# Reading three chunks of x once, transposed, instead of twice, in a fused decoder layer on one core

## The chip, the cores and the metric

The kernel runs on one core of a Trainium2 chip. The core has a matrix engine (PE in the profile, with its weight loads as PEld), VectorE (DVE), ScalarE (ACT), GpSimd (POOL), and SyncE (SP), which here only issues DMAs. The metric is the device time of one execution in microseconds (us). A trace of the profiled execution gives the span from the first to the last instruction; the execution's own time is a little longer.

## The reference

One decoder layer over 2048 rows of 1024 values, all in f32. Cut to what matters here:

```python
u = rmsnorm(h, norm_g)                 # x * rsqrt(mean(x*x) + 1e-6) * gain, row by row
proj = jnp.einsum('bsd,de->bse', u, w_in)      # 1024 -> 4096 columns
a_q, a_f, a_i, a_g, b_q, b_k, b_v, b_g = split(proj)      # 8 x 512
o_a = head_rmsnorm(hgrn2(...), ...) * silu(a_g)           # group A: 4 heads
o_b = head_rmsnorm(stick_breaking(b_q, b_k, b_v), ...) * silu(b_g)   # group B: 8 heads
h = h + concat(o_a, o_b) @ w_out
h = h + sigmoid(rmsnorm(h) @ w_ple_gate) * rmsnorm(p @ w_ple_proj)
return rmsnorm(h, final_norm)
```

The change touches the first line only: the root mean square of each row of x, and the normalised x in the layout that the projection wants.

## The kernel before

**Tiles and units.** The rows of x stand reversed in memory, in NC = 4 chunks of 512 rows (CH), each of CB = 4 blocks of 128. The projection's 4096 columns stand as 8 groups of 512 (B and A in turn). The main loop (L825) goes over 32 units, one group and one chunk each, group by group and the chunks from 3 down to 0. So units 0 to 3 are group 0 of B on chunks 3, 2, 1, 0: they need the four chunks of normalised x one after the other, and every later unit finds them all ready. All values go to the PE as two f16 parts, high and low: `xh[c]`, `xl[c]` for x, `w.h`, `w.l` for weights (shown as wh and wl). One product is then three matmuls, xh with wh, xl with wh, xh with wl (`passes`, L347). Per unit these are 48 matmuls of 512 columns for two transposed outputs (`proj_t`, here q and k) and 96 of 256 columns for two natural ones (`proj_n`, here v and the gate), all summed in PSUM tiles called pj (three of them).

**Normalising a chunk.** A chunk is held as 8 slices, k = 0 to 7, each of 128 values of the model dimension on the partitions and 512 rows along the free dimension. Chunk 3 has a path of its own (`prep_first`, L263), which the change leaves alone; its last block goes through two DMA transposes (L222, xh<-kq_t and xl<-fa_t). Chunks 2, 1 and 0 go through `prep_x` (L224):

- The chunk is read in natural order, 8 tiles of 256 KB (L230). ACT squares each and sums along the row in the same instruction (L231, with an instruction that reads the accumulator), and one DVE reduction (L243) gives `ss`, a sum for each row.
- `rsqrt` (L79) makes v on DVE (L83) and raises it to -1/2 on POOL (L84). The result has rows on the partitions and must be spread over all partitions: DVE scales the identity with it (dg, L247) and four f32 matmuls of a matrix of constants with dg (L251, 128 columns each) put it into the PSUM tile `bc`, which ACT copies to SBUF (L253).
- The chunk is read again, transposed, as 4 pairs of slices of 512 KB (L238, tag kq, two buffers), and each slice is multiplied (DVE, L258), rounded to f16 (ACT, L259) and subtracted for the low part (L260, DVE for even k, POOL for odd).

**What sets the order.** The generators are tasks. `spawn` puts one on a list with a unit by which it must be done; `run` advances tasks between the matmuls of a unit by an estimated clock, and `drain` finishes what is due. Unit 0 spawns `prep_x` for chunks 2 and 1, unit 1 for chunk 0 (L829): each chunk's task starts at least one unit ahead of the unit that uses it. The order in which each engine gets its instructions is then settled by the scheduler when the program is built; on the chip every engine takes its own in that order, and waits where an operand or a buffer is not ready. SP issues all DMAs in order from one queue.

**What runs beside it.** Every B unit spawns a mixer task (`mix_B`, L593), four blocks of it. A block has score matmuls z (from q, kept in qs_t, and keys in bkv, both written by 64 KB DMAs from SBUF to SBUF, L448 and L457, after the unit's q and k are split), two sigmoids (ACT, L616 and L617), a scan (DVE, L621, 642 long), a product (L626), f16 parts (ACT L629, POOL L631 and L633), a DMA transpose (L635, at_t<-wt_t) and output matmuls op. Each unit also loads and splits two slices of the next group's weights (L128, L132, L133).

The tags of `prep_x` in the change (kq, fa, kp0, kp1, sc, raw) are buffers that the kernel has already; the mixer of group A uses kq, fa, kp0 and kp1 from unit 4 on.

## Time and profile before

| what | value |
|---|---|
| median of 3 runs | 1259.12 us (1257.2 to 1259.24) |
| profiled execution, own time | 1259.13 us |
| its span | 1257.4 us |
| busy: PE, DVE, ACT, POOL | 96%, 69%, 47%, 28% of the span |
| mean granted PE clock | 0.987 of full speed |
| HBM read | 60.83 MB |

The shares are means over stages that differ. In the profile each engine has its own rows, and a row says how long it was busy and what ended the idle time ahead of it. A wait counts for the end only on the engine that is never idle afterwards; here that is the PE. A granted clock of 1.00 is the PE's 2.4 GHz; its other level is 1.2 GHz.

### The profile page before, as it was taken

The numbers are of one execution on the slowest core, as the hardware profiler recorded it, in microseconds if no ns is written. First come the engines' busy times: TensorE is split into PE (matmuls) and PEld (weight loads), VectorE is DVE, ScalarE is ACT, GpSimd is POOL, SyncE is SP. The second block draws the span as 40 slices with busy tenths as digits, with TensorE's granted clock in tenths as the row PEclk, the third lists the DMA queues.
The fourth block names the chain that finished last, engine by engine and source line by source line (L and its number), as shares of the span: only waits on it lengthen the run. The fifth ranks groups of instructions, "written<-read, shape, count | busy, mean of one in ns | idle before, by whom it ended". The sixth has DMA issues, their size and how long they took to land.

```text
span 1257.4 us, 25854 instructions
## 1 busy us (share of the span) xinstructions
PE 1211.4 (96%) x9802; PEld 775.9 (62%) x9802; DVE 870.4 (69%) x1736; ACT 596.4 (47%) x1507; POOL 355.0 (28%) x472
## 2 busy tenths in 40 slices
PE   7978999999999999999999999898999999999997
PEld 7655667667766777677677766665544444444443
DVE  5769799976589995579997558998854434344233
ACT  7556544544454454464454445564533333333222
POOL 4247451114442112444111444110021211111212
PEclk9999999999999999999999999899999999999999
DMA  9896731156661035772126565357644536336211
GB/s 258 260 224 172 173 106 32 41 149 145 152 147 29 19 116 145 156 179 54 27 67 142 133 156 116 129 161 200 139 82 117 151 84 162 106 108 145 59 51 53
DMA packets 258468, 155.42 MB, mean 124 GB/s; under 512 B 181280, under 2 KB 226336, under 8 KB 258336
## 3 DMA queue, kind: packets, MB, share of 16 engines
q1 hardware_dynamic: 258192, 153.43, 49.1%
q8 instruction: 79, 1.29, 0.4%
q14 instruction: 53, 0.43, 0.1%
q10 hardware_dynamic: 144, 0.26, 0.1%
HBM read 60.83 MB, written 33.55 MB: 75 GB/s over the span
## 4 chain that ended last, share of the span: by engine, by line
PE 71%; DVE 11%; DMA 9%; ACT 4%; issue 3%; POOL 2%; SPq 1%; POOLq 0%; DVEq 0%; ACTq 0%
PE pj L160 35%; PE np L160 28%; PE op L160 3%; PE lps L160 2%; DVE wl L133 2%; PE z L160 2%; DMA at_t<-wt_t 2%; DVE e_t L621 1%; DMA at_t<-kp_t 1%; DMA raw_t<-w_in 1%; DMA raw_t<-x_nat 1%; DVE kq_t L511 1%; ACT wh L132 1%; DMA raw_t<-w_out 1%; DVE e_t L626 1%
## 5 line engine op out<-in xcount | busy, mean ns | idle before, releaser
L160 PE MATMUL pj<-wh,xh 128*128 128x256 f16 x1024 | 282.1, 275 | 2.0 <-DVE ql_t L77 2.0
L160 PE MATMUL pj<-wh,xl 128*128 128x256 f16 x1024 | 282.1, 275 | 0.0
L160 PE MATMUL pj<-wl,xh 128*128 128x256 f16 x1024 | 282.0, 275 | 0.0
L160 PEld LDWEIGHTS <-xh 128*128 128x128 f16 x2048 | 201.6, 99 | 28.3 <-issue 0.3
L160 PE MATMUL pj<-xh,wh 128*128 128x512 f16 (+1 forms) x560 | 197.0, 363 | 4.4 <-ACT xh L76 2.2
L160 PE MATMUL pj<-xl,wh 128*128 128x512 f16 (+1 forms) x560 | 197.5, 362 | 2.3 <-DVE xl L260 1.7
L160 PE MATMUL pj<-xh,wl 128*128 128x512 f16 (+1 forms) x560 | 197.4, 362 | 0.0
L84 POOL TENSOR_TENSOR rs_y<-rs_v,mhalf 128x1 f32<-128x1 f32 (+2 forms) x87 | 77.4, 891 | 288.9 <-DVE rs_v L83 288.0
L160 PE MATMUL np<-wh,fy 128*128 128x512 f16 x512 | 156.4, 379 | 0.2 <-DVE e_t L732 0.2
L160 PEld LDWEIGHTS <-wh 128*128 128x128 f16 x1120 | 100.4, 98 | 88.5 <-issue 6.8
L160 PEld LDWEIGHTS <-at_t 128*128 128x128 f16 x1688 | 100.4, 98 | 84.7 <-DMA at_t<-wt_t 14.2
L160 PEld LDWEIGHTS <-fy 128*128 128x128 f16 x768 | 74.2, 98 | 87.9 <-issue 0.6
L160 PEld LDWEIGHTS <-xl 128*128 128x128 f16 x1024 | 101.2, 99 | 17.7 <-issue 2.5
L160 PE MATMUL np<-wh,at_t 128*128 128x512 f16 (+2 forms) x264 | 98.0, 373 | 0.0
L160 PE MATMUL np<-wl,at_t 128*128 128x512 f16 (+2 forms) x264 | 98.0, 373 | 0.0
L160 PE MATMUL np<-wh,wt_t 128*128 128x512 f16 (+2 forms) x264 | 97.9, 373 | 0.0
L160 PE MATMUL np<-wl,fy 128*128 128x512 f16 x256 | 97.1, 379 | 0.0
L621 DVE TENSOR_TENSOR_SCAN e_t<-e_t,reset 128x642 f32<-128x642 f32 x56 | 85.4, 1524 | 15.8 <-ACT e_t L616 15.2
L629 ACT CAST wt_t<-e_t 128x640 f16<-128x640 f32 (+1 forms) x64 | 44.7, 698 | 104.7 <-DVE e_t L626 88.8
L160 PEld LDWEIGHTS <-wl 128*128 128x128 f16 x560 | 54.0, 99 | 59.4 <-issue 2.7
L631 POOL TENSOR_TENSOR wt_t<-e_t,wt_t 128x512 f16<-128x512 f32 (+1 forms) x64 | 78.0, 1218 | 33.5 <-ACT wt_t L629 32.9
L764 DVE TENSOR_TENSOR e_t<-e_t,kq_t 128x512 f32<-128x512 f32 (+2 forms) x33 | 22.2, 674 | 92.7 <-POOL kq_t L763 92.6
(193 smaller groups left out, 2270.9 us busy)
## 6 DMA issues: line engine op xcount, KB each, us to landing
raw_t<-w_in SPq DMA_DIRECT2D x61, 256.0 KB, 3.8
raw_t<-x_nat SPq DMA_DIRECT2D x56, 256.0 KB, 3.9
y_d<-y_t SPq DMA_DIRECT2D x32, 256.0 KB, 2.6
yn<-y_d SPq DMA_DIRECT2D x16, 512.0 KB, 4.0
out<-y_t SPq DMA_DIRECT2D x31, 256.0 KB, 2.1
kq_t<-x_t SPq DMA_DIRECT2D x12, 512.0 KB, 5.1
bkv<-kn_t SPq DMA_DIRECT2D x64, 64.0 KB, 2.3
bkv<-ql_t SPq DMA_DIRECT2D x64, 64.0 KB, 2.0
```

What stands on the lines that cost most here:

```text
L84: nc.gpsimd.tensor_tensor(y, v, mhalf[:, 0:n], op=ALU.pow)
L132: nc.scalar.activation(self.h[:, k, :], self.r[k], AF.Copy, scale=g)
L133: nc.vector.scalar_tensor_tensor(self.l[:, k, :], self.r[k], g, self.h[:, k, :], op0=ALU.mult, op1=ALU.subtract)
L160: nc.tensor.matmul(out_, lhsT, rhs, start=start, stop=stop)
L511: nc.vector.tensor_tensor(act, act, other, op=ALU.mult)
L621: nc.vector.tensor_tensor_scan(fl(pr_), fl(f), fl(reset), 0.0, op0=ALU.mult, op1=ALU.max)
L626: nc.vector.tensor_tensor(sg[:, :, :w_], sg[:, :, :w_], pr_[:, :, :w_], op=ALU.mult)
L629: nc.scalar.copy(wt[:, :, :w_], sg[:, :, :w_])
L631: nc.gpsimd.tensor_tensor(wt[:, :, 3 * P : 3 * P + lw], sg[:, :, :lw], wt[:, :, :lw], op=ALU.subtract)
L764: nc.vector.tensor_tensor(h_, h_, p_, op=ALU.add)
```

## The change

`prep_x` no longer reads the natural rows. It loads all 8 transposed slices of a chunk (two pairs into kq, four single slices into fa, fa, kp0, kp1), squares each on ACT, and adds the squares into two accumulators of 128 x 512 (tag sc), even k on DVE and odd k on POOL; one more DVE add joins them. A row's sum now lies across the partitions, so four matmuls with the accumulator's blocks as weights and one column of the constant matrix (L249, one output column each) bring it to the layout that `rsqrt` wants, in the first four columns of `bc`. The constant in that matrix is a power of two, which the scale of `rsqrt` takes out. From there on the steps are the same, except that all 8 slices are in SBUF already. Chunk 2's task starts in unit 0, as before; chunk 1's is spawned when chunk 2's is through, and chunk 0's after chunk 1's.

```diff
     def prep_x(c):
-        ss = small("ssx", CB, 2)
-        hs_ = small("ssx2", 2 * CB, 2)
+
+        xt = {}
+        for k in (0, 2):
+            pair = f32("kq", (P, 2, CH))
+            nc.sync.dma_start(pair, x_t[c, :, k : k + 2, :])
+            xt[k], xt[k + 1] = pair[:, 0, :], pair[:, 1, :]
+        for k in range(4, KD):
+            xt[k] = f32(("fa", "fa", "kp0", "kp1")[k - 4])
+            nc.sync.dma_start(xt[k], x_t[c, :, k, :])
+            yield 0.5
+        acc = []
+        for k in range(KD):
+            sq = f32("sc") if k < 2 else raw("sq")
+            nc.scalar.activation(sq, xt[k], AF.Square)
+            if k < 2:
+                acc.append(sq)
+            else:
+                (nc.gpsimd if k % 2 else nc.vector).tensor_tensor(acc[k % 2], acc[k % 2], sq, op=ALU.add)
+            yield 0.8
+        nc.vector.tensor_tensor(acc[0], acc[0], acc[1], op=ALU.add)
+        yield 2.0
+        bc = pa("bc")
+        ss = bc[:, 0:CB]
         for b in range(CB):
-            for hf in range(2):
-                xn = raw("xn")
-                nc.sync.dma_start(xn, x_rows(c, b, hf))
-                nc.scalar.activation(xn, xn, AF.Square, accum_out=hs_[:, 2 * b + hf : 2 * b + hf + 1])
-            yield 1.0
...
-        r = rsqrt(ss, CB, 1.0 / D, EPS)
+            nc.tensor.matmul(ss[:, b : b + 1], acc[0][:, b * P : (b + 1) * P], ones[:, 0:1], start=True, stop=True)
+        r = rsqrt(ss, CB, 1.0 / D * p2(-SX), EPS)
...
+        if c > 0:
+            spawn(prep_x(c - 1), 0.0, -1)
...
-        for n in ([c - 1, c - 2] if u == 0 else [c - 2]):
-            if g == 0 and n >= 0:
-                spawn(prep_x(n), 0.0 if n == c - 1 else 12.0, 1)
+        if u == 0:
+            spawn(prep_x(c - 1), 0.0, 1)
```

The scheduler's order moves with it. Two places matter; in all of them names carry buffer numbers. From the PE's first matmul of unit 4 on, the order on the PE is the same in both kernels.

PE, before: the broadcast of chunk 1's factors (bc_770) stands among the first projection matmuls of unit 1, which work on chunk 2 (xh_514, xl_515); chunk 1 itself (xh_783) comes into use only with unit 2, some 260 rows further on.

```order
L160 MATMUL pj_898<-xh_514,wh_126 128x512
L251 MATMUL bc_770<-dg_738,ones_89 128x128
L251 MATMUL bc_770<-dg_772,ones_89 128x128
L160 MATMUL pj_839<-xl_515,wh_126 128x512
L160 MATMUL pj_839<-xh_514,wl_127 128x512
...
L251 MATMUL bc_770<-dg_775,ones_89 128x128
L251 MATMUL bc_770<-dg_778,ones_89 128x128
...
L160 MATMUL pj_1232<-xh_783,wh_126 128x512
```

PE, the change: the same chunk's sums (L249) and factors (bc_983) stand in the last quarter of unit 1's projection (pj_1011 is its last tile), and the second half of the factors behind a score tile of unit 1's own mixer (z_1183); only score matmuls stand between it and the first matmul of unit 2 (pj_1152, on chunk 1 as xh_1048).

```order
L249 MATMUL bc_983<-ones_89,sc_t_806 128x1 x4
L160 MATMUL pj_1011<-wl_127,xh_673 128x256
...
L256 MATMUL bc_983<-dg_1037,ones_89 128x128
...
L160 MATMUL z_1183<-bkv_318,qs0_t_753 128x128
...
L256 MATMUL bc_983<-dg_1040,ones_89 128x128
L256 MATMUL bc_983<-dg_1043,ones_89 128x128
L160 MATMUL z_1184<-bkv_318,qs1_t_754 128x128
...
L160 MATMUL z_1384<-bkv_317,qs1_t_754 128x320
L160 MATMUL pj_1152<-xh_1048,wh_126 128x512
```

What moved: the spreading of chunk 1's factors went from the head of unit 1 to its end, so the matmuls that used to stand between it and chunk 1's first use are now ahead of it. Chunk 0, with bc_1420 and unit 3, stands in the same way; chunk 2's factors stand at the very end of unit 0.

DVE, before: chunk 1's first slices (kq_t_729, low part xl_784) among the scans (L624, L626) of unit 0's mixer, ahead of the splits of unit 1's q.

```order
L258 TENSOR_TENSOR y_t_787<-kq_t_729,sc_t_781 128x512
L258 TENSOR_TENSOR y_t_805<-kq_t_729,sc_t_781 128x512
L624 SCALAR_TENSOR_TENSOR e1_t_845<-e1_t_845,reset_311 128x129
L260 TENSOR_TENSOR xl_784<-y_t_787,xh_783 128x512
L626 TENSOR_TENSOR e0_t_844<-e0_t_844,e1_t_845 128x2x128
L258 TENSOR_TENSOR y_t_811<-kq_t_731,sc_t_781 128x512
L77 SCALAR_TENSOR_TENSOR ql_t_836<-pj_839,qh_t_835 128x512
```

DVE, the change: chunk 1's first slices (kq_t_760, low part xl_1049) stand behind the splits of unit 1's outputs (bkv_319, gs_t_913), and two full scans (L627) with a product (L632) stand between the first multiplication and the first low part.

```order
L253 TENSOR_SCALAR dg_1043<-ident_84,rs_y_989 128x128
L77 SCALAR_TENSOR_TENSOR bkv_319<-pj_1011,bkv_319 128x256
L262 TENSOR_TENSOR y_t_1050<-kq_t_760,sc_t_1046 128x512
L262 TENSOR_TENSOR y_t_1082<-kq_t_760,sc_t_1046 128x512
L388 SCALAR_TENSOR_TENSOR gs_t_913<-pj_1011,gs_t_913 128x256
L627 SCALAR_TENSOR_TENSOR e1_t_1180<-e1_t_1180,reset_311 128x642
L627 SCALAR_TENSOR_TENSOR e1_t_1289<-e1_t_1289,reset_311 128x642
L632 TENSOR_TENSOR e0_t_1179<-e0_t_1179,e1_t_1180 128x640
L264 TENSOR_TENSOR xl_1049<-y_t_1050,xh_1048 128x512
```

What moved: the multiplications of a chunk went from one unit ahead of its use to the moment of its use, and the first low part stands behind 642-long scans.

## Rows read from the trace of the kernel before

**Rows 1.** Busy time by stretch (units 0 to 3, the rest); count in brackets; clock, DMA share.

```profile
12.44:46.44 34.00, 29.56 (x329) 27.62 (x329) 19.97 (x45) 25.48 (x67) 7.81 (x11) 0.90 0.92 262
46.44:73.55 27.11, 23.82 (x176) 16.63 (x174) 23.93 (x36) 16.11 (x41) 10.14 (x12) 1.00 0.88 240
73.55:106.25 32.70, 29.06 (x222) 19.97 (x220) 22.02 (x32) 17.51 (x42) 15.85 (x17) 0.90 0.81 195
106.25:141.22 34.97, 28.25 (x258) 19.50 (x256) 27.98 (x31) 17.38 (x39) 23.72 (x31) 0.95 0.67 165
141.22:1257.40 1116.18, 1093.21 (x8782) 685.08 (x8779) 770.98 (x1584) 511.65 (x1305) 287.56 (x373) 0.99 0.46 112
```

**Rows 2.** PE's waits from 0 to 142 us: total, times, longest.

```profile
PE op L160 <- DMA at_t<-wt_t: 9.0, 4, 3.3
...
PE pj L160 <- DMA xh<-kq_t: 2.2, 1, 2.2
PE pj L160 <- DVE ql_t L77: 2.0, 1, 2.0
...
PE z L160 <- DMA bkv<-ql_t: 1.6, 1, 1.6
```

**Rows 3.** Stretches in which the granted clock was low (the third last column).

```profile
30.00:36.30 6.30, 4.62 (x39) 4.27 (x39) 1.09 (x5) 1.29 (x4) 0.14 (x1) 0.73 0.85 259
91.50:98.00 6.50, 6.45 (x46) 5.14 (x47) 3.59 (x6) 3.23 (x7) 0.14 (x2) 0.53 0.77 219
128.30:132.00 3.70, 3.63 (x31) 2.86 (x32) 1.96 (x2) 3.02 (x7) 2.10 (x5) 0.54 0.70 142
```

**Rows 4.** DMA issues from 0 to 150 us: KB each, median us to landing.

```profile
raw_t<-x_nat SPq DMA_DIRECT2D x24, 256.0 KB, 4.4
...
bkv<-ql_t SPq DMA_DIRECT2D x16, 64.0 KB, 2.2
```

**Rows 5.** ACT's groups from 0 to 140 us, by form: busy, mean ns, idle before.

```profile
L231 ACT ACTIVATE raw_t<-raw_t 128x512 f32<-128x512 f32 x24 | 15.1, 631 | 12.9 <-DMA raw_t<-x_nat 12.9
...
L616 ACT ACTIVATE e_t<-z 128x320 f32<-128x320 f32 x20 | 8.8, 445 | 5.3 <-PE z L160 4.7 <-POOL flag L628 0.6
...
L231 ACT ACTIVATION_READ_ACCUMULATOR raw_t<-raw_t 128x1 f32 x24 | 4.7, 195 | 0.0
```

**Rows 6.** The chain of waits: start, us, what (two transposes of 8x128 blocks).

```profile
23.81 7.57 DMA xh<-kq_t
...
192.16 3.92 DMA at_t<-kp_t
```

**Rows 7.** DVE's groups from 0 to 140 us, by form.

```profile
L258 DVE TENSOR_TENSOR y_t<-kq_t,sc_t 128x512 f32<-128x512 f32 x24 | 21.3, 907 | 9.6 <-ACT sc_t L253 7.1 <-DMA kq_t<-x_t 1.6 <-POOL e_t L609 0.9
L621 DVE TENSOR_TENSOR_SCAN e_t<-e_t,reset 128x642 f32<-128x642 f32 x10 | 16.8, 1677 | 1.6 <-ACT e_t L616 1.6
L626 DVE TENSOR_TENSOR e_t<-e_t 128x640 f32<-128x640 f32 x9 | 9.3, 1028 | 0.4 <-issue 0.2
L260 DVE TENSOR_TENSOR xl<-y_t,xh 128x512 f16<-128x512 f32 x12 | 8.5, 712 | 1.6 <-ACT xh L259 1.5
```

**Rows 8.** DVE's timeline, the multiplications of two slices, twice.

```profile
39.25 1.29 DVE L258 TENSOR_TENSOR y_t<-kq_t,sc_t 128x512 f32<-128x512 f32 x2 [3.91 <-ACT sc_t L253]
...
101.37 2.41 DVE L258 TENSOR_TENSOR y_t<-kq_t,sc_t 128x512 f32<-128x512 f32 x2
```

**Rows 9.** POOL's timeline beside the second of those.

```profile
100.22 2.18 POOL L631 TENSOR_TENSOR wt_t<-e_t,wt_t 128x512 f16<-128x512 f32 x1
```

**Rows 10.** POOL's groups from 0 to 140 us, by form.

```profile
L260 POOL TENSOR_TENSOR xl<-y_t,xh 128x512 f16<-128x512 f32 x12 | 16.0, 1336 | 30.3 <-ACT xh L259 30.3
```

**Rows 11.** The tile bc: duration in ns, least, median, most; first and last start.

```profile
L251 PE MATMUL bc<-dg,ones x24: 272/275/562, 33.9 to 93.3; 128*128 128x128 f32 x24
L253 ACT COPY sc_t<-bc x3: 566/586/586, 38.7 to 93.8; 128x512 f32<-128x512 f32 x3
```

**Rows 12.** SP's timeline: four of the eight key copies of a unit.

```profile
97.66 2.41 SPq L457 DMA_DIRECT2D bkv<-kn_t  x4
```

More of the change, by code (lines that the diff above doesn't have):

```diff
@@ L224, in prep_x @@
     def prep_x(c):
-        ss = small("ssx", CB, 2)
-        hs_ = small("ssx2", 2 * CB, 2)
-        for b in range(CB):
-            for hf in range(2):
-                xn = raw("xn")
-                nc.sync.dma_start(xn, x_rows(c, b, hf))
-                nc.scalar.activation(xn, xn, AF.Square, accum_out=hs_[:, 2 * b + hf : 2 * b + hf + 1])
-            yield 1.0
-        xt = {}
-        def load_t(k):
-            if k < KD and k % 2 == 0:
-                pair = f32("kq", (P, 2, CH))
-                nc.sync.dma_start(pair, x_t[c, :, k : k + 2, :])
-                xt[k], xt[k + 1] = pair[:, 0, :], pair[:, 1, :]
-        for k in range(4):
-            load_t(k)
-        nc.vector.tensor_reduce(ss, hs_.rearrange("p (b h) -> p b h", h=2), axis=AX, op=ALU.add)
-        r = rsqrt(ss, CB, 1.0 / D, EPS)
+        xt = {}
[20 more added lines that the diff above has]
+        ss = bc[:, 0:CB]
+        for b in range(CB):
+            nc.tensor.matmul(ss[:, b : b + 1], acc[0][:, b * P : (b + 1) * P], ones[:, 0:1], start=True, stop=True)
+        r = rsqrt(ss, CB, 1.0 / D * p2(-SX), EPS)
         for b in range(CB):
@@ L249, in prep_x @@
                 yield 3.0
-                bc = pa("bc")
             nc.tensor.matmul(bc[:, b * P : (b + 1) * P], ones, dg, start=True, stop=True)
@@ L255, in prep_x @@
         for k in range(KD):
-            load_t(k + 4)
             xs = f32("y")
```

## The prediction

> **What bounds the kernel now.** I read busy time by stretch first. From the first matmul of unit 4, at 141.22 us, to the end the PE is busy 1093.2 of 1116.2 us [rows 1], and the order of its work there is the same in both kernels. So the change can show only in when the PE gets to that matmul; what it loses or gains before then is passed on whole. Ahead of it, from the first projection matmul at 12.44 us, lie units 0 to 3: 128.8 us, in which the PE is idle 4.4 + 3.3 + 3.6 + 6.7 = 18.1 us (length less busy in each stretch of rows 1). The waits say for what: 9.0 us for the mixer's transposes at_t, 2.2 for the transpose of chunk 3's last block, 2.0 for a pj buffer that DVE has still to empty, 1.6 for key copies [rows 2]. Behind three of these waits the granted clock falls to its lower level, 1.2 GHz, for a while: length times missing share is 6.30 x 0.27 + 6.50 x 0.47 + 3.70 x 0.46 = 6.5 us lost [rows 3]. What is left is work at full clock: 128.8 - 18.1 - 6.5 = 104.2 us. So at most 24.6 us are there to win, some 2%, and DVE is near by: busy 28.0 of 35.0 us in unit 3, against the PE's 28.3 [rows 1].
>
> **What is removed.** 24 loads of 256 KB, 6.3 MB, of a stretch in which the DMA engines are 67% to 92% busy [rows 1, 4]. On ACT the squares stay, 24 at 0.63 us, but the 24 accumulator reads of 0.195 go, 4.7 us [rows 5]; ACT is not the bound (at most 25.5 of 34.0 us [rows 1]), so I cost that at nothing by itself. It does help once: before, six squares stand on ACT ahead of the last block of chunk 3, so its transposes can go some 2.5 us earlier. The transpose took 7.57 us among the loads, against 3.92 for one of the same shape in a quiet stretch [rows 6]. Both together are more than the PE's 2.2 us wait, so that wait goes, and with it the first clock fall, 1.7 us.
>
> **What is added on the PE.** Twelve one-column f32 matmuls. The nearest row is the broadcast with 128 columns: two records of 0.275 us per matmul, which overlap [rows 11]. That puts one between nothing and 0.55 us; I take 0.25, nearer the middle than the columns alone would say, since the weights are as large as there: 12 x 0.25 = 3.0 us (0 to 6.6).
>
> **What is added on DVE and POOL.** Per chunk 4 adds on DVE and 3 on POOL, all of 128 x 512 with two SBUF inputs. The multiplication of a slice is DVE's nearest row: 1.29 us for two with POOL idle [rows 8], 2.41 for two with POOL at work [rows 8, 9], 0.907 in the mean [rows 7]. So 12 adds are 8 to 14 us of DVE, and 9 on POOL are 12 us at 1.34 each [rows 10]. They are done while the PE has the previous chunk, so they cost nothing in themselves, as long as DVE has slack in that unit; where it has none they come on top (the third rival). The Trainium skill, in SBUF — State Buffer, section Who interferes with whom, says that a DVE instruction with two SBUF inputs and a GpSimd instruction that reads SBUF share a read interface, and that the one that comes later waits until the first is through. That speaks against adds on POOL next to multiplications on DVE. The trace agrees in kind: 2.41 us against 1.29 for the same two multiplications [rows 8, 9]. By the rule alone each of the nine adds could hold DVE for its length, 12 us in all. The sum below takes the mean of rows 7, 0.907, which has POOL's share of today in it.
>
> **What is moved: the lead is gone.** Before, chunk 1 is normalised during unit 1 and used in unit 2. In the change a chunk's buffers are free only when it has been multiplied, the sums come late in the unit, and the factors stand at the end of the unit ahead of the use. From there to the first low part of the chunk there is a chain with little for the PE to do. I work out what is left uncovered before each chunk:
>
> - Chunk 2: four broadcast matmuls behind the last matmul of unit 0 (1.1 us, with dg between them), two short sigmoids (0.5; 0.445 each at 320 columns, here 128 [rows 5]), copy 0.59 [rows 11], two multiplications 1.29 [rows 8], three short scans of 643 columns together (1.7, as one of 642 [rows 7]), a short product (0.5), the low part 0.71 [rows 7]: 6.4 us. In it lie the broadcasts and 12 score matmuls, 2.8 us. Uncovered: 3.6.
> - Chunk 1: copy 0.59, two pairs of sigmoids ahead of it (0.8), multiplications 1.29, the gate's product 0.4 (half of the 0.71 for 512 columns), two scans at 1.68, a product 1.03, the low part 0.71: 8.2 us. Score and output matmuls cover 2.3. Uncovered: 5.9.
> - Chunk 0: copy and sigmoids 1.5, multiplications 1.3, product 1.0, one scan 1.7, low part 0.7: 6.2, less 1.8 of PE work. Uncovered: 4.4.
>
> The first high part is there some 2 to 4 us before the first low part, but the PE's order wants the low part as the second matmul of each tile. The second half of the factors of chunks 1 and 0 stands behind score matmuls, which need the unit's keys: after the split (1.2 us) 14 issues of 64 or 128 KB at 2.41 / 4 = 0.6 us [rows 12] and 2.2 us to land [rows 4], 11.8 us. The PE has behind the split of unit 1 the other three eighths of the projection (7.7), the new matmuls (1.0) and 1.9 of scores and outputs, 10.6 us, and a little less in unit 2: 2.5 us of waits for both.
>
> With the chunk's parts coming while they are used, DVE's pace counts too. The PE needs 12.9 us for a chunk's 8 slices (72 of the unit's 144 matmuls, five eighths of some 20.6 us, a unit's busy time less scores and outputs [rows 1]) and 1.9 for output matmuls. DVE has, from the first low part to the last, 6 multiplications, 3 subtractions, 2 or 3 scans and products, 12 to 16 us [rows 7]. I take 0.9, 0.6 and 2.7 us of waits in units 1, 2 and 3: 4.2.
>
> **The sum.** Idle: 2.0 (the pj buffer, as before) + 3.6 + 5.9 + 4.4 + 2.5 + 4.2 = 22.6. With less DMA traffic I keep one of the four waits for at_t, 9.0 / 4 = 2.2. Before, the clock fell behind three of the longer waits, though not behind the longest (3.3 us, in unit 1, whose clock is 1.00 [rows 1, 2]); I let it fall behind each of the three new ones, 6.5 us as in rows 3. Half of that lies under DVE's pace, so 3.2 count. Together 28.0, against 24.6 before; with 3.0 of new work the matmul of unit 4 comes at 12.4 + 104.2 + 3.0 + 28.0 = 147.6 instead of 141.2. That is 6.4 us later. The profiled execution took 1259.1 us, as the median of the runs did (1259.1): 1265.5 us. The ends: without at_t waits, clock falls, and price for the new matmuls, with the scans out of the way of the low parts (3.4) and 2.0 less of DVE's pace, it is 13.8 less, 1251.7. With all four at_t waits (6.8 more), the whole clock loss (3.3), the new matmuls at 0.55 (3.6) and half of the 24 multiplications at 1.2 (3.6) it is 17.3 more, 1282.8.
>
> **The rivals.**
>
> 1. *Faster: the transfers were the trouble.* All waits that end with a DMA are 12.8 us [rows 2], and the clock falls come behind them. If the lighter DMA load takes them all away and the chains above are half as long, because the scans are through when the factors come, the uncovered 13.9 us become 7, and 2.2 and 3.2 go: 12.3 less than the forecast, 1253. The point is 2.5 us uncovered per chunk: below that the change wins. For it: DMA at 92% in unit 0. Against it: the order on DVE and PE is fixed, and puts the scans there. Chance 0.25.
> 2. *No change.* The holes cost what the transfers give back: 1259, chance 0.15.
> 3. *Slower by more: DVE becomes the bound.* Unit 3 had 28.0 us of DVE work in 35.0 [rows 1]. The adds (4 in each of units 0 to 2) and POOL's adds, if each of the nine holds DVE for its 1.34 us, bring 8 + 12 us over three chunks; a third of it shows: 6 to 7 us more, 1272. By the rule of the Trainium skill named above it would be this case. The trace so far shows the mean multiplication at 0.907, not at the 1.2 of rows 8's second row, so I give it 0.2.
>
> My forecast has 0.4, with a range of its own of 1262 to 1269. So 0.25 faster, 0.15 the same, 0.6 slower, where 0.2% (2.5 us) is about what a measurement of this kernel tells from no change. The range for 8 in 10 takes in most of rivals 1 and 3: 1252 to 1276.
>
> **What would show it.** In the profile after: unit 4's first matmul at about 147 us; no wait of the PE for xh<-kq_t; three idle stretches ahead of units 1, 2 and 3, ended by a low part (DVE) or the copy of bc (ACT), of about 4, 6 and 4 us; HBM read down by 6.3 MB; the granted clock low behind those stretches; DVE busier in units 1 and 2 than before. I am wrong if those waits are under 2.5 us each (rival 1), if DVE is busy throughout and the PE waits in small pieces within the units (rival 3), or if the time after unit 4's start changes by more than 2 us.

## The result, and the profile after

The change is slower: 1286.08 us (median of 4 runs, 1283.50 to 1293.20) against 1259.09 (4 runs of the kernel before), a ratio of 1.0224 with a 95% interval of 1.0202 to 1.0246. The forecast had the sign, but 6.4 us where 27.0 were lost, and the time lies above its range. The profiled execution took 1283.5 us with a span of 1281.8 and is the shortest of the four. HBM reads fell from 60.83 to 54.54 MB, as they should.

The busy times by stretch, as in [rows 1], for the change: units 0 to 4 and all that follows, each unit from its first projection matmul (ahead of it some early matmuls at 14.43 us; the first stretch begins at 12.44 to match the kernel before).

```profile
12.44:48.92 36.48, 30.11 (x350) 27.43 (x349) 23.46 (x48) 19.89 (x48) 9.48 (x12) 0.97 0.54 164
48.92:83.82 34.90, 29.11 (x219) 19.29 (x218) 29.35 (x37) 20.70 (x46) 18.11 (x20) 0.95 0.63 165
83.82:125.03 41.21, 31.33 (x259) 20.52 (x258) 36.61 (x44) 23.05 (x49) 28.12 (x29) 0.96 0.69 182
125.03:158.51 33.48, 25.55 (x209) 16.35 (x207) 21.49 (x23) 11.49 (x23) 22.00 (x21) 0.95 0.45 112
158.51:188.67 30.16, 24.54 (x199) 16.59 (x197) 26.12 (x40) 17.42 (x39) 13.82 (x16) 1.00 0.50 143
188.67:1281.80 1093.13, 1069.80 (x8557) 667.97 (x8555) 742.57 (x1545) 493.49 (x1265) 271.64 (x355) 0.99 0.44 108
```

The same view of the kernel before, for unit 4 and what follows:

```profile
141.22:167.29 26.07, 25.05 (x226) 17.44 (x224) 22.87 (x31) 16.51 (x35) 13.26 (x16) 1.00 0.84 208
167.29:1257.40 1090.11, 1068.16 (x8558) 667.64 (x8555) 748.11 (x1554) 495.14 (x1271) 274.30 (x358) 0.99 0.45 109
```

Unit 4 starts at 158.51 instead of 141.22, 17.3 us later, where 6.4 were forecast. Unit 4 itself loses 30.16 - 26.07 = 4.1 more, and the rest of the span 3.0: together the 24.4 by which the span grew. Unit 4 loses this with less work in it: the PE's order in the two kernels is the same only from unit 5 on (its last few matmuls apart, unit 4 differs), not from unit 4 on, as the section on the change has it. Of the output matmuls (op) unit 4 holds 64 before (first row) and 36 in the change; the other 28, some 1 us, stand ahead of it there and are part of the 17.3.

```profile
141.22:167.29 26.07, 2.53 (x64) 0.00 (x0) 0.58 (x1) 1.00 0.84 208
...
158.51:188.67 30.16, 1.56 (x36) 0.68 (x1) 0.59 (x1) 1.00 0.50 143
```

DVE (the third pair of numbers in the rows of all work) is busy 29.35 of 34.90 us in unit 1 and 36.61 of 41.21 in unit 2, and its work from 12.44 us to unit 4 went from 93.9 to 110.9 us (sums of [rows 1] and of the first four rows here).

What the PE waited for, from 12.44 us to the end of unit 4, in the change:

```profile
PE op L160 <- DMA at_t<-wt_t: 12.6, 7, 4.1
PE pj L160 <- DVE xl L264: 9.6, 7, 2.5
PE pj L160 <- DVE ql_t L77: 4.6, 3, 3.2
PE z L160 <- DMA bkv<-ql_t: 2.7, 3, 1.5
PE bc L256 <- DVE dg L253: 2.4, 4, 1.3
```

and the largest of the kernel before, in the stretch that answers to it (12.44 to 167.29 us):

```profile
PE op L160 <- DMA at_t<-wt_t: 10.0, 5, 3.3
```

The wait for xh<-kq_t [rows 2] is gone, as forecast. The waits for at_t are not: 12.6 us instead of 10.0, though the DMA engines are now 45% to 69% busy in units 0 to 3. A transpose can come late because it lands slowly or because it is issued late. The longest landing before and the longest wait in the change show one of each (SyncE's issue, then the PE's matmul with its wait; before first):

```profile
83.13 2.84 SPq L635 DMA_TRANSPOSE at_t<-wt_t  x1
...
91.55 0.66 PE L160 MATMUL op<-bkv,at_t 128*128 128x64 f16 x9 [2.67 <-DMA at_t<-wt_t]
...
183.93 1.33 SPq L641 DMA_TRANSPOSE at_t<-wt_t  x1
...
187.30 0.64 PE L160 MATMUL op<-bkv,at_t 128*128 128x64 f16 x16 [4.08 <-DMA at_t<-wt_t]
```

From 300 to 700 us of the kernel before the median from issue to landing is 3.4 us. The five transposes that the PE waited for before took 5.6, 5.2, 8.4, 4.2 and 6.7 us; had each taken 3.4, an estimated 7 of the 10.0 us would not have been waited. In the change the seven took 4.0, 3.9 and five times 3.3 to 3.4: slow landing accounts for some 1 of 12.6 us. So the lighter traffic did take the old waits away, and new ones came, for transposes that are issued late.

The three long holes for low parts did not come as such; they came as seven waits for low parts (xl) of at most 2.5 us, within the units.

DVE's groups of instructions in the change, from 12.44 to 158.51 us (they answer to [rows 7]):

```profile
L264 DVE TENSOR_TENSOR xl<-y_t,xh 128x512 f16<-128x512 f32 x12 | 11.2, 934 | 0.7 <-ACT xh L263 0.7
L242 DVE TENSOR_TENSOR sc_t<-sc_t,raw_t 128x512 f32<-128x512 f32 x9 | 9.8, 1092 | 6.5 <-ACT raw_t L238 6.3
L262 DVE TENSOR_TENSOR y_t<-kq_t,sc_t 128x512 f32<-128x512 f32 x12 | 9.1, 799 | 1.0 <-ACT sc_t L258 1.0
...
L262 DVE TENSOR_TENSOR y_t<-fa_t,sc_t 128x512 f32<-128x512 f32 x6 | 8.6, 1459 | 0.0
...
L244 DVE TENSOR_TENSOR sc_t<-sc_t 128x512 f32<-128x512 f32 x3 | 2.0, 678 | 0.0
```

The adds (L242 and the joins, L244) are 11.8 us; the subtractions for the low parts went from 0.712 to 0.934 us each. And the timeline of DVE and POOL in unit 3 shows how the two meet:

```profile
125.63 1.58 DVE L264 TENSOR_TENSOR xl<-y_t,xh 128x512 f16<-128x512 f32 x1
127.13 0.67 DVE L667 TENSOR_REDUCE ssB<-sc_t 128x8 f32<-128x512 f32 x1
127.73 1.32 DVE L632 TENSOR_TENSOR e_t<-e_t 128x640 f32<-128x640 f32 x1
128.98 1.51 DVE L262 TENSOR_TENSOR y_t<-kq_t,sc_t 128x512 f32<-128x512 f32 x2
130.41 1.12 DVE L83 TENSOR_SCALAR rs_v<-ssB 128x8 f32<-128x8 f32 x1
131.45 1.48 DVE L627 TENSOR_TENSOR_SCAN e_t<-e_t,reset 128x642 f32<-128x642 f32 x1
133.07 0.83 DVE L632 TENSOR_TENSOR e_t<-e_t 128x640 f32<-128x640 f32 x1
133.81 0.69 DVE L264 TENSOR_TENSOR xl<-y_t,xh 128x512 f16<-128x512 f32 x1
...
136.41 1.77 DVE L632 TENSOR_TENSOR e_t<-e_t 128x640 f32<-128x640 f32 x1
...
135.85 1.65 POOL L264 TENSOR_TENSOR xl<-y_t,xh 128x512 f16<-128x512 f32 x1
```

DVE never rests in these 12 us, yet between two low parts of chunk 0 (125.63 and 133.81) stand the products, the scan and the statistics of unit 2's mixer. Without a lead, a chunk's normalising and the mixer of the unit before it want DVE at the same time, and the PE has to wait for both.

### The profile page after: what moved, and what is told of

The parts are those of the page before. It is cut to its first block, busy times and chain, and to the rows that moved or that the text cites. A ratio compares the mean times of both kernels' runs of the same rounds, so it can differ in the third digit from the quotient of the medians.

```text
span 1281.8 us, 25877 instructions
## 1 busy us (share of the span) xinstructions
PE 1217.8 (95%) x9826; PEld 775.2 (60%) x9826; DVE 884.8 (69%) x1745; ACT 594.6 (46%) x1483; POOL 371.6 (29%) x481
## 3 DMA queue, kind: packets, MB, share of 16 engines
HBM read 54.54 MB, written 33.55 MB: 69 GB/s over the span
## 4 chain that ended last, share of the span: by engine, by line
PE 70%; DVE 11%; DMA 8%; issue 4%; ACT 3%; POOL 2%; SPq 1%; POOLq 0%; DVEq 0%; ACTq 0%
PE pj L160 35%; PE np L160 27%; PE op L160 3%; PE lps L160 2%; DVE wl L133 2%; PE z L160 2%; DVE e_t L627 1%; DMA raw_t<-w_in 1%; DVE y_t L262 1%; DMA at_t<-wt_t 1%; DMA raw_t<-w_out 1%; ACT wh L132 1%; DMA yn<-y_d 1%; DVE kq_t L517 1%; DMA at_t<-kp_t 1%
## 5 line engine op out<-in xcount | busy, mean ns | idle before, releaser
L627 DVE TENSOR_TENSOR_SCAN e_t<-e_t,reset 128x642 f32<-128x642 f32 x56 | 85.3, 1524 | 14.4 <-ACT e_t L622 14.2
```

The costliest lines, as they stand in the source:

```text
L627: nc.vector.tensor_tensor_scan(fl(pr_), fl(f), fl(reset), 0.0, op0=ALU.mult, op1=ALU.max)
```

## The experiments

Two theories. **A**: the lost lead makes the loss. **B**: the adds make it, as work on DVE and through what POOL's adds do to DVE. In the table, "less before" is the median less that of the kernel before on the same chip in the same session (1259.6 to 1260.6 us there, 1259.1 for the change).

| run | what it is | median | less before | ratio, 95% interval |
|---|---|---|---|---|
| change | | 1286.1 | +27.0 | 1.0224 (1.0202 to 1.0246) |
| e1 | lead for chunks 1 and 0 | 1271.6 | +11.1 | 1.0089 (1.0068 to 1.0111) |
| e2 | change without the six adds | 1282.0 | +21.5 | 1.0171 (1.0146 to 1.0196) |
| e3 | before, spawned as the change | 1258.4 | -2.1 | 0.9985 (0.9972 to 0.9999) |
| e4 | change, all adds on DVE | 1284.9 | +24.4 | 1.0198 (1.0175 to 1.0221) |
| e5 | lead for chunks 2 and 1 | 1263.0 | +2.5 | 1.0015 (1.0004 to 1.0027) |
| e6 | e5 without the six adds | 1255.9 | -4.6 | 0.9964 (0.9949 to 0.9979) |
| e7 | e5, sums on the PE | 1255.0 | -5.5 | 0.9956 (0.9940 to 0.9972) |
| e8 | before, 21 loads fewer | 1258.7 | -1.8 | 0.9985 (0.9971 to 0.9999) |
| e9 | change, two slices spare | 1286.7 | +26.3 | 1.0221 (1.0194 to 1.0247) |
| e10 | chunks in place, adds | 1258.1 | -2.4 | 0.9981 (0.9971 to 0.9992) |
| e11 | chunks in place, sums on the PE | 1256.7 | -3.8 | 0.9969 (0.9957 to 0.9980) |
| e12 | change, sums on the PE | 1277.7 | +17.2 | 1.0141 (1.0123 to 1.0158) |
| e13 | change, third sc buffer | 1285.9 | +25.3 | 1.0194 (1.0171 to 1.0216) |
| e14 | e9 and e13 together | 1288.3 | +27.7 | 1.0226 (1.0202 to 1.0249) |
| e15 | lead for all, adds | 1263.7 | +3.1 | 1.0024 (1.0011 to 1.0038) |
| e16 | lead for all, sums on the PE | 1256.6 | -4.0 | 0.9969 (0.9955 to 0.9983) |
| e17 | e12, two slices spare | 1274.4 | +14.8 | 1.0114 (1.0087 to 1.0142) |
| e18 | buffers of e1, spawned as the change | 1277.2 | +17.6 | 1.0133 (1.0103 to 1.0164) |

### The lead given back in part, and its two halves: e1, e3, e18

```diff
+        if c == 1:
+            for i, tag in enumerate(("xh0", "xl0")):
+                big = xpool.tile([P, 4, CH], F32, name="xr", tag=tag)
+                for k in (0, 2):
+                    nc.sync.dma_start(big[:, k : k + 2, :], x_t[c, :, 4 * i + k : 4 * i + k + 2, :])
+                for k in range(4):
+                    xt[4 * i + k] = big[:, k, :]
...
-        if u == 0:
-            spawn(prep_x(c - 1), 0.0, 1)
+        for n in ([c - 1, c - 2] if u == 0 else [c - 2]):
+            if g == 0 and n >= 0:
+                spawn(prep_x(n), 0.0 if n == c - 1 else 12.0, 1)
```

> The changed kernel with the lead restored: chunk 1's eight slices are held as f32 in the 16 KB that chunk 0's xh and xl take later, the sc tag gets one buffer more, and the tasks are spawned as in the kernel before (chunks 2 and 1 in unit 0, chunk 0 in unit 1). Reads, squares, adds and one-column matmuls stay as in the change. Theory A (the lost lead makes the 27 us): the uncovered chains ahead of units 2 and 3 go, so unit 4 starts at 137 to 146 us (141.2 before, 158.5 in the change) and the time is 1254 to 1264. Theory B (the adds and the port that DVE and POOL share make most of it): the same adds are there, only earlier, so 1272 to 1284.

The run also has a third sc buffer, and the spawn at the end of `prep_x` goes. Measured 1271.6: between the two theories, 15.9 of 27.0 us back. e3 is the kernel before with the second half of this diff the other way round, e18 has the first half alone (and the sc buffer).

> The kernel before, with only the spawning of the change: chunk 1's task is spawned when chunk 2's is through, chunk 0's after chunk 1's. The natural rows are still read and summed on ACT. In the built order the factors of chunk 1 then stand some 30 matmul rows later than before, those of chunk 0 some 45, and still a good way ahead of their unit. Theory A as 'the spawning alone takes the lead': 1275 to 1290. Theory A as 'the buffers take the lead, because a chunk's sums can start only when the chunk ahead has left kq, fa and kp': 1257 to 1264, about as before. Theory B: about as before, too.

> The first run with the lead restored gave chunk 1 buffers of its own and spawned the tasks early (1271.6). This one has its buffers (chunk 1 in the space of chunk 0's xh and xl, third sc buffer) and the change's spawning, each task behind the one ahead. If the buffers alone give the lead back, as the run with the spawning alone suggests, which cost nothing: 1269 to 1275. If the early spawning is needed too, because the sums of chunks 1 and 0 still come late: 1278 to 1286.

e3 measured 1258.4: the spawning costs the kernel before nothing, since a natural chunk can be summed long before its transposed slices have a buffer. e18 measured 1277.2, between the two cases: the buffers alone give back 9.4 us, the early spawning on top 6.5. So it is first the buffers that took the lead: a chunk read once must stay on chip from its squares to its multiplication.

### Is it the adds? e2, e4, e12

```diff
-                (nc.gpsimd if k % 2 else nc.vector).tensor_tensor(acc[k % 2], acc[k % 2], sq, op=ALU.add)
+                pass
```

> The changed kernel without the six accumulating adds of a chunk (three on DVE, three on POOL); the joining add and the eight squares stay. The sum of squares then covers two of the eight slices only, the other six are left out. Theory A (lead): the sums come some 2 us earlier per chunk, the chain from the factors to the low part stays: 1276 to 1284. Theory B (adds): with nine adds on DVE of 0.7 to 1.75 us and nine on POOL of 1.28 gone, 1260 to 1270.

Measured 1282.0, 5.5 us gained, in A's range. e4 puts the line's adds on `nc.vector` for every k:

> The changed kernel with all adds on DVE: six adds of about 0.7 us and the join per chunk, none on POOL. Theory A (lead): the last add comes some 1 us earlier or later, so no change to speak of, 1283 to 1289. Theory B as 'POOL's adds hold DVE's port': 9 x 1.28 us of holding go, 9 x 0.7 us of adds come, 1278 to 1283. Theory B as 'DVE's own work is the bound': nine more adds of 0.7 us on DVE, 1287 to 1293.

Measured 1284.9: no difference that counts. e12 goes further than e2 and sums on the PE; the adds, their join and the four f32 matmuls go:

```diff
+            sq = wk.tile([P, CH], F16, name="sq", tag="raw", bufs=5)
             nc.scalar.activation(sq, xt[k], AF.Square)
+            for b in range(CB):
+                nc.tensor.matmul(ss[:, b : b + 1], sq[:, b * P : (b + 1) * P], ones16[:, 0:1],
+                                 start=k == 0 and b == 0, stop=k == KD - 1 and b == CB - 1)
```

> The changed kernel, spawns and buffers as they are, with the sums on the PE in place of all adds (f16 squares, 32 one-column matmuls per chunk). Theory A (the ring of the buffers): the ring loses the adds' link, about 2 us per chunk as in the run without adds: 1276 to 1283. Theory B (the adds): at most 1270.

Measured 1277.7, in A's range. All adds together, with the accumulators' buffers and the join that go with them, are worth 27.0 - 17.2 = 9.8 us without a lead; 17.2 stay without any add. In e12 DVE is busy 30.76 of 39.60 us in unit 2, less than in the change, and the unit is still 6.9 us longer than before (first row; the second is unit 4):

```profile
79.37:118.97 39.60, 34.55 (x310) 22.99 (x310) 30.76 (x40) 23.77 (x52) 19.05 (x26) 0.89 0.69 175
...
150.51:181.23 30.72, 26.32 (x208) 17.76 (x206) 25.69 (x39) 17.41 (x39) 13.12 (x16) 0.94 0.55 146
```

### The lead of chunk 2, with and without adds: e5, e6, e7

e5 is e1 with `if c == 2`, e6 adds the diff of e2 to it, e7 that of e12. Chunk 2 then needs none of the buffers that chunk 3's last block holds in unit 0.

> As the run with the lead restored, but the 16 KB of chunk 0's xh and xl hold chunk 2's eight slices, and chunks 1 and 0 go through kq, fa, kp0 and kp1. Chunk 2's loads then need no buffer that chunk 3's last block holds. Reads, squares, adds and one-column matmuls are those of the change. In the run before this one unit 0 took 37.3 us and unit 1 35.7 (34.0 and 27.1 in the kernel before). Theory A (what was left there is the lead that chunk 2 still lacked): unit 1 comes back to 27 to 30 us and the time is 1258 to 1265. Theory B (what was left is the adds): 1268 to 1274.

> The kernel with the lead for chunk 2, without the six accumulating adds per chunk; the sum of squares then covers two of the eight slices, the other six are left out. Theory A (with a lead the adds lie beside other work): within 3 us of the same kernel with the adds. Theory B (adds and port): 6 us or more below it.

> The kernel with the lead for chunk 2, with all adds of the sums moved to the PE: ACT writes each square as f16, and four one-column matmuls per slice (32 per chunk, with the square's blocks as weights) sum the slices in PSUM. The squares are rounded to f16, everything else is as in the change. At 0.1 us for a matmul with f16 weights (0.11 is the spacing of the projection's 128-wide ones) the PE gets 3 x (3.2 - 1.0) = 6.6 us more than with the adds. Theory A: 3 to 7 us over the kernel with the lead for chunk 2. Theory B: the adds that go are worth more than that, so the same or less.

e5 measured 1263.0, as A had it; but e6 and e7 measured 1255.9 and 1255.0, 7 and 8 us less, as B had it. Both theories hold a part. The 96 one-column matmuls of e7 cost the PE little (first line; the second is e7's unit 4):

```profile
L250 PE MATMUL bc<-ones,sq 128*128 128x1 f16 x96 | 5.0, 164 | 0.9 <-ACT sq L248 0.8
...
133.51:158.39 24.88, 24.88 (x227) 17.52 (x224) 22.57 (x34) 15.92 (x36) 12.96 (x15) 1.00 0.76 193
```

5.0 us for 96, 0.052 each, half of what I had put down.

### The transfers alone: e8

```diff
-                xn = raw("xn")
-                nc.sync.dma_start(xn, x_rows(c, b, hf))
-                nc.scalar.activation(xn, xn, AF.Square, accum_out=hs_[:, 2 * b + hf : 2 * b + hf + 1])
+                if b == 0 and hf == 0:
+                    xn = raw("xn")
+                    nc.sync.dma_start(xn, x_rows(c, b, hf))
+                nc.scalar.activation(raw("jk_"), xn, AF.Square, accum_out=hs_[:, 2 * b + hf : 2 * b + hf + 1])
```

> The kernel before with one natural tile of eight read per chunk: ACT still squares and sums eight times with the same instructions, always the same tile, so 7 of the 8 natural tiles are left out of the sums. 21 loads of 256 KB go, 5.5 MB; all order and work else stays. It prices what the change's lighter traffic is worth by itself. Rival 1 of the prediction (the transfers are the trouble): most of the 12.8 us of waits that end with a DMA go, and clock with them: 1245 to 1251. Otherwise: 1254 to 1260.

Measured 1258.7, 1.8 us gained. Its waits, to the end of unit 4, and its unit 0:

```profile
PE op L160 <- DMA at_t<-wt_t: 9.7, 5, 3.1
PE pj L160 <- DVE ql_t L77: 5.4, 1, 5.4
...
PE pj L160 <- DMA xh<-kq_t: 0.2, 1, 0.2
...
12.44:48.37 35.93, 29.55 (x333) 26.47 (x333) 21.64 (x52) 29.16 (x81) 7.89 (x11) 0.90 0.62 162
```

The lighter traffic takes the wait for xh<-kq_t away, 2.2 to 0.2, and leaves those for at_t, 9.7 us. But the run does not price the transfers as cleanly as it was meant to. The loads that go stood mostly in unit 0, where the DMA share falls from 0.92 to 0.62; in units 1 to 3, where the waits for at_t stand, it is 0.86, 0.83 and 0.63, against 0.88, 0.81 and 0.67 before. So it does not test whether the load makes those late. The built order moved as well, and what unit 0 gained at its first wait it lost at a new one, 5.4 us for a split that stands on DVE behind chunk 2's factors. Unit 4 starts at 136.59, 4.6 us early; the median keeps 1.8 of it.

### A theory that fell: the ring of buffers, e9, e13, e14, e17

In the change a chunk's first multiplications start at 46.57, 81.04 and 122.31 us: 34.5 and 41.3 apart, the lengths of units 1 and 2. I took that for a ring, in which the last load waits for the release of kp1 and everything else for that load. The change's timeline from chunk 1's last slices to chunk 0's factors, ACT, POOL, then DVE:

```profile
102.06 0.62 ACT L238 ACTIVATE sc_t<-kq_t 128x512 f32<-128x512 f32 x1
...
106.91 0.63 ACT L238 ACTIVATE raw_t<-kp_t 128x512 f32<-128x512 f32 x1 [2.58 <-DMA kp_t<-x_t]
...
107.69 1.26 POOL L242 TENSOR_TENSOR sc_t<-sc_t,raw_t 128x512 f32<-128x512 f32 x1 [1.07 <-ACT raw_t L238]
...
109.27 0.68 DVE L244 TENSOR_TENSOR sc_t<-sc_t 128x512 f32<-128x512 f32 x1
...
115.97 1.26 DVE L253 TENSOR_SCALAR dg<-ident,rs_y 128x128 f32<-128x128 f32 x2 [0.83 <-POOL rs_y L84]
...
122.31 1.27 DVE L262 TENSOR_TENSOR y_t<-kq_t,sc_t 128x512 f32<-128x512 f32 x2
```

The last square waits 2.58 us for its load. Cutting that, e9:

```diff
+            if c == 1 and k >= 6:
+                if k == 6:
+                    spare = xpool.tile([P, 2, CH], F32, name="spare", tag="xh0")
+                xt[k] = spare[:, k - 6, :]
+            else:
+                xt[k] = f32(("fa", "fa", "kp0", "kp1")[k - 4])
```

> The changed kernel, but chunk 1's last two slices (k = 6, 7) go into 4 KB of the space that chunk 0's xh takes later, so that kp0 and kp1 are free for chunk 0's long before. Spawns, adds, sums stay; the PE's order is nearly that of the change. Ring theory: with one set of buffers a chunk's multiplications, the release, the next chunk's last loads, squares, adds, sums and factors follow each other, and the ring sets the length of units 1 and 2 (from first multiplication to first multiplication 34.5 and 41.3 us in the change, the units 34.9 and 41.2). The last load of chunk 1 then goes with fa's release, some 2 us earlier (62.8 instead of 65.0), that of chunk 0 some 4 us (98 instead of 102.6): 1278 to 1283. Theory that DVE and POOL are simply full there: nothing changes for them, 1284 to 1288.

Measured 1286.7, no gain. In its trace the last square came at 104.68, but the square of k = 1 still came only at 102.49, since it needs the sc buffer that holds the factors of the chunk ahead, and POOL's three adds stood behind that. So e13 gave sc a third buffer (`sc=3`), e14 both:

> The changed kernel with a third sc buffer, nothing else; the PE's order is that of the change. In the change the second accumulator (square of k = 1) waits for the sc buffer of the previous chunk's factors: it comes at 102.06 us, after that chunk's last multiplication, and POOL's three adds of 1.3 to 1.5 us after it. Ring theory: the other link, the last load for kp1, still lands only for a square at 106.9, and its add ends at 109.0 as now: no change, 1283 to 1288. Full engines: no change either.

> The changed kernel with both links cut: chunk 1's last two slices in spare space, so that the last loads of chunks 1 and 0 don't wait for kp0 and kp1, and a third sc buffer, so that the adds don't wait for the factors of the chunk ahead. Ring theory: chunk 0's joined sum comes 2 to 3 us earlier (about 107 instead of 109.3), chunk 1's 1 to 2 us, and the units follow: 1279 to 1283, though each cut alone gave or should give nothing. Full engines: 1284 to 1288.

e13 measured 1285.9 as expected, e14 1288.3: the ring theory fell. e14's timeline, POOL and then DVE, tells where the cut ran dry:

```profile
102.88 3.04 POOL L247 TENSOR_TENSOR sc_t<-sc_t,raw_t 128x512 f32<-128x512 f32 x2 [0.31 <-ACT raw_t L243]
...
104.72 1.75 DVE L269 TENSOR_TENSOR xl<-y_t,xh 128x512 f16<-128x512 f32 x1
106.50 0.69 DVE L267 TENSOR_TENSOR y_t<-spare,sc_t 128x512 f32<-128x512 f32 x1
107.11 0.68 DVE L247 TENSOR_TENSOR sc_t<-sc_t,raw_t 128x512 f32<-128x512 f32 x1
...
108.98 0.68 DVE L249 TENSOR_TENSOR sc_t<-sc_t 128x512 f32<-128x512 f32 x1
```

POOL's last add ended at 105.9 instead of 108.9. But two of DVE's own adds, a weight split and a slow low part (1.75 us) now stood ahead of chunk 1's last multiplication, which moved from 100.82 to 106.50, and the join came at 108.98 instead of 109.27. With the adds, DVE's order is the limit in this trace, not the buffers. e17 is e12 with the two spare slices, the same cut with no add on any engine:

> The kernel with the sums on the PE and no lead (1277.7), with chunk 1's last two slices in spare space, so that the last loads of chunks 1 and 0 don't wait for kp0 and kp1. There are no accumulators and no adds, so the last load is the only link left between a chunk's last multiplication and the next chunk's sums. If the release of the buffers limits there: 2 to 4 us per chunk, 1270 to 1275. If a chunk is held by the order of work on DVE and ACT behind its sums and not by its loads: 1276 to 1280.

Measured 1274.4, 3.3 us less than e12 as medians (2.4 less before): just inside the first range. Without the adds the release of the buffers seems to cost a little; the intervals of the two runs overlap.

### Every chunk with its lead, and what beats both: e10, e11, e15, e16

e10 loads chunks 2, 1 and 0 into the bytes of their own xh and xl:

```diff
+            x16[c] = xpool.tile([P, KD, 2 * CH], F16, name="x16", tag=f"x{c}")
+            xh[c], xl[c] = x16[c][:, :, 0:CH], x16[c][:, :, CH : 2 * CH]
...
+            nc.sync.dma_start(x16[c][:, k : k + 2, :].bitcast(F32), x_t[c, :, k : k + 2, :])
+            for j in (k, k + 1):
+                xt[j] = x16[c][:, j, :].bitcast(F32)
```

> Chunks 2, 1 and 0 are loaded as f32 into the very bytes that take their own xh and xl (slice k: 2 KB, of which the high part takes the first half and the low part the second once the slice has been multiplied). No buffer is shared between chunks any more; spawns as in the kernel before, one more sc buffer; reads, squares, adds and one-column matmuls as in the change. In the built order the first factors of chunk 3 stand on DVE as in the kernel before again. Theory A (the lost lead is the whole loss): chunk 0's lead comes back too, with it the 4 to 5 us lost in unit 4, and the 2 us at the start: 1253 to 1259. Theory B (the adds keep costing some 7 us): 1259 to 1265.

e11 is e10 with the diff of e12.

> As the run with the chunks loaded in place, with the sums on the PE (f16 squares from ACT, 32 one-column matmuls per chunk) in place of all adds. With the adds the worth of 7 us that the two runs with chunk 2's lead showed: 1246 to 1253, the fastest of all. If the adds are hidden once every chunk has its lead: within 3 us of the run with the adds.

e10 measured 1258.1: the change's reads, squares, adds and sums, with its buffers and spawns changed, 28.0 us below the change (29.4 by the column less before) and 0.19% below the kernel before (0.08 to 0.29). A's range. (The "2 us at the start" were no loss: after the early matmuls the projection goes on at 15.55 us in the change and at 16.15 before.) e11 measured 1256.7, less of a gain than hoped. That the sums come a unit earlier does not explain it by itself: 9 of DVE's 12 adds start in unit 0 in e10, and 8 of 12 in e15, where the adds cost 7.1 us (below). e15 and e16 give every chunk its lead with the buffers of e5 for chunks 2 and 1, and load only chunk 0 in place:

> Every chunk with its lead, without the joint buffers of the in-place run for chunks 2 and 1: chunk 2's slices in the 16 KB of chunk 0's xh and xl, chunk 1's in kq, fa, kp0 and kp1, chunk 0's in place in its own xh and xl once chunk 2 has been multiplied. Third sc buffer; adds as in the change. Against the run with chunk 2's lead (1263.0), where unit 4 still took 31.7 us against 26.1 in the kernel before, chunk 0's lead should take that loss away: unit 4 at 26 to 27 us, 1256 to 1260. If the loss in unit 4 has another cause: 1261 to 1265.

> As the run with every chunk's lead, with the sums on the PE (f16 squares, 32 one-column matmuls per chunk) and no adds. Against 1255.0 for the sums on the PE with chunk 2's lead: 1249 to 1254 if chunk 0's lead is worth anything there, 1254 to 1257 if the output part eats it, as it ate 8 of the 9 us by which unit 4 started earlier in the in-place run.

e15 measured 1263.7, no better than e5, although unit 4 lost nothing any more, 26.46 us against 31.67 in e5:

```profile
140.51:172.18 31.67, 26.69 (x227) 18.25 (x224) 26.24 (x40) 18.17 (x40) 14.38 (x20) 0.95 0.68 171
...
141.00:167.46 26.46, 25.06 (x227) 17.43 (x225) 22.40 (x35) 16.35 (x37) 14.19 (x15) 1.00 0.68 170
```

(first row e5, second e15). In e15's profiled execution all after unit 4 took 5.4 us longer than in the kernel before (1263.0 - 167.46 against 1090.1). The traces place 3.6 of it: unit 29 starts 0.8 us later (776.03 against 775.25), the last matmul of group A's scores (lps) 4.4 us later (910.9 against 906.5), and from 760 to 940 us the PE waits 13.4 us, where it waited 10.8. Why is open. e16 measured 1256.6, its second case, beside e7. The fastest is e7, 0.44% below the kernel before (0.28 to 0.60): x read once, sums on the PE with squares rounded to f16, chunk 2 in space that is used later.

## Why the prediction was wrong

**Right**: the sign; the cause that it put first, the lead; the read bytes; the one-column matmuls (eight records in 0.95 to 1.05 us, four matmuls at 0.25); the wait for xh<-kq_t, which went, in e8 too, so the transfers were its cause; and the load behind the old waits for at_t, which went too. Rival 1's time was rightly held unlikely, though e8, with 1.8 us for 21 loads, leaves the load of units 1 to 3 untested.

The sum's terms, put together by what they stand for: the lead 13.9 uncovered + 2.5 for keys + 4.2 of DVE's pace = 20.6; new matmuls 3.0; adds nothing; and against it old idle and clock of 24.6 less the 2.0, 2.2 and 3.2 that were kept, 17.2 gained. 20.6 + 3.0 - 17.2 = 6.4. Against the runs:

- **The lead, 20.6: about right in size, in part by luck.** The change less e5 is 24.5 us with the adds, e12 less e7 22.7 without (with chunk 0's lead too 23.9 and 29.4 with them, by e15 and e10, 21.2 and 21.0 without, by e16 and e11). But unit 4 starts only 18.0 and 17.0 us earlier in e5 and e7; some 6 us come after it, where the forecast had nothing. The kind was partly wrong: I expected three holes ahead of units 1 to 3; what came was many small waits within the units, the sign that the prediction gave for its third rival.
- **The adds "cost nothing in themselves, as long as DVE has slack in that unit": failed.** They cost 9.8 us without a lead (change less e12) and 8.0 or 7.1 with it (e5 less e7, e15 less e16). With the PE's part taken the same (5.0 us of matmuls in e7 against 3.0) they are about 2 more. I had priced them, 8 to 14 us on DVE, and laid them under a slack that the moved multiplications of the next chunk needed too. The third rival had this mechanism, with a third of its 20 us showing; about half showed. Only in e10 do they cost little (1.4, against e11), which no run explains.
- **"With less DMA traffic I keep one of the four waits for at_t": failed.** Kept were 2.2 us; in the change 7.0 come ahead of unit 4 and 5.6 in it, and they are new ones, for transposes issued late. The sum had no term for what the lost lead does to the mixer. The clock was a smaller miss: by length times missing share in units 0 to 3 the change loses 1.1 + 1.7 + 1.6 + 1.7 = 6.1 us, the kernel before 8.4 [rows 1], of which the 6.5 of the prediction leave out the first 3.3 us (12.44 to 15.70, granted clock 0.50); so 2.3 us were gained where 3.3 were forecast. The best version of the read-once kernel, e7, gains 5.5 us in all, some 10 if its sums cost nothing; not 17.
- **"What it loses or gains before then is passed on whole": failed by 7 us of the change's 24.4.** Its ground was that the PE's order is the same from unit 4 on; it is the same from unit 5 on. Unit 4 took 30.16 us instead of 26.07. It took 26.3 to 27.3 in the five kernels where chunk 0 has its lead (e1, e10, e11, e15, e16), and 28.8 to 31.8 without, but for e7 (24.9). Without the lead unit 3's q and k are split late (k at 151.35 us, 7.2 before unit 4; 11.5 in the kernel before). Its mixer stands in unit 4 in both kernels, but in the change its first scores are ordered behind 21 projection matmuls instead of 11, and the PE then waits 5.6 us for at_t (1.0 before), 4.1 at the longest. The other 3.0 come late: unit 29 starts 20.9 us later than before (796.13 against 775.25), the last matmul of group A's scores 24.0 later (the last start in these lines, before first):

```profile
L160 PE MATMUL lps<-qch_t,kp_t x896: 190/193/261, 170.5 to 906.5; 128*128 128x64 f16 x180
...
L160 PE MATMUL lps<-qch_t,kp_t x896: 190/193/258, 193.5 to 930.5; 128*128 128x64 f16 x180
```

  The order there is the same; e10 loses 3.5 us in that stretch, e15 3.6, e5 and e7 nothing. Nor are gains passed on: e10 starts unit 4 at 132.06, 9.2 us early, and its span ends 1.2 early.

So the number failed by 20.6 us: 9.8 for the adds, 8.7 for gains that did not come (5.5 in e7, its sums included, for 17.2 - 3.0 = 14.2), 2.1 for the lead. By place, in one execution of each kernel, the miss is 10.9 us ahead of unit 4 (adds 8.0, gains 6.5, the lead 3.6 less than forecast, from the starts of unit 4 in the change, e12 and e7), 7.1 behind it, and 2.6 by which the change's profiled execution lies below its median. Rows of the trace before could have warned of the first [rows 1, 7]: added to the 23.9 and 22.0 us that DVE worked in units 1 and 2, four adds each and the multiplications that moved in brought it to 29.4 of 34.9 and 36.6 of 41.2.

The Trainium skill, SBUF — State Buffer, section Who interferes with whom, has a DVE instruction with two SBUF inputs contend with a GpSimd instruction that reads SBUF: the one that starts later waits until the other is through. The trace agrees in kind: DVE's adds took 1.092 us in the mean in the change, 0.677 at the least, and 0.782 in the mean in e4, which has none on POOL. e4's expectation put the holds at 5 us, nine adds of POOL at 1.28 less nine more on DVE at 0.7; it gained 1 to 3, and the intervals of the two overlap. DVE's work to unit 4 is 111.3 us in e4 and 110.9 in the change, so the nine adds brought DVE as much as the holds had.

**What stays open**: how the 23 us of the lead divide among DVE's order, the late factors and the clock (the ring of buffers explains 3 at most, e17), why the adds cost 7 us in e15 and 1.4 in e10, and why the change, e10 and e15 lose some 3.5 us from unit 29 to the last scores.

## What to carry to other kernels

Reading data once instead of twice saves bytes but lengthens its life: between its statistics and its use it holds buffers, and if those are the buffers of the tile before it, the lead is lost. Look first for space that is written only later, and load there, even into the bytes of the result (e10). Work "beside" an engine's other work counts as free only after it has been added to what else the change moves into the same stretch. And a loss is passed on whole only where the order is the same, so compare the order from the very place on where the sum stops.

## What the runs showed that I had not expected

- The same line of the waits, PE <- DMA at_t, had two causes: slow landings in the kernel before (up to 8.4 us), late issues in the change (landing in 3.3 to 4.0 us). Only the time from issue to landing tells them apart.
- A sum over partitions by one-column matmuls with f16 weights cost 0.052 us each (5.0 us for 96), and 0.25 with f32 weights, where the nearest row, 128 columns in f32, is 0.275 for each of two records.
- Moving nine adds of 128x512 from POOL to DVE changed nothing that can be measured: 1284.9 and 1286.1 us.
